# One-hot rows for eight tokens per instruction, as four interleaved pairs

## The chip, the cores and the metric

The kernel runs on one core of one Trainium2 chip. The metric is the device time of one execution in microseconds. A core has five engines that run beside each other, each with its own queue, in order: TensorE (PE, matmuls; its weight loads are shown as PEld), VectorE (DVE), ScalarE (ACT), GpSimd (POOL) and SyncE (SP, which here only issues transfers). They meet at semaphores. The lines L... are lines of the kernel before.

## The reference, cut to what matters

The kernel computes two transformer blocks on 512 tokens of width 1024. The change lies in the first block's expert layer, which picks 128 of 16,384 small experts per token (8 heads of 16) and sums their outputs:

```python
def peer_ffn(h, w_q, sub_keys, u, v):
    ...
    idx = jnp.take_along_axis(cand_idx, pos, axis=-1)     # i1 * 128 + i2
    g = jax.nn.softmax(top_s, axis=-1)
    ...
        ue = jnp.take(u, ib, axis=0)
        a = jnp.einsum('thkd,td->thk', ue, xb, preferred_element_type=jnp.float32)
        w = jax.nn.gelu(a) * gb
        ve = jnp.take(v, ib, axis=0)
        return jnp.einsum('thk,thkd->td', w.astype(ve.dtype), ve)
```

## The kernel before

The kernel gathers nothing. It multiplies all 16,384 rows of u with all tokens, weights each result with the gate of that expert for that token (zero for nearly all), and multiplies with all of v. An expert's number is a pair (i1, i2), each below 128. So the gates of one token are a 128 x 128 matrix, the sum over the 128 picks of an outer product of one-hot rows: a matmul over the picks, with a matrix of one-hot rows of i2 as the loaded operand and one-hot rows of i1, times the gate, as the moving one.

In `weights_of_pairs` (L1060 to L1085) VectorE builds these for one token at a time, the 128 picks on the partitions. L1073 compares `iotah` (0 to 127) with the token's column of `its` and gives `o2`; L1074 and L1076 compare with the other column and multiply by the high and the low half of the gate (`gts`), which give `g0` and `g1`. All three are 128x128 in 16 bits. Two matmuls at L1080 (PE, out `ax`) add up a token's matrix, four tokens share a PSUM bank (three `ax` banks), ScalarE copies the bank into `sg` at L1082, and after 32 tokens L1085 sends `sg` (2 MB) to the DRAM tensor `gdr`. The tiles `o2`, `g0` and `g1` hold four tokens and have four buffers each. In the trace they appear as o and g.

Beside it `up` (from L916) multiplies the tokens with u in units. A unit's weight is loaded by SyncE (L175, two buffers), rounded by ScalarE (L178, `wh`), its remainder `wl` is taken by GpSimd for the first units and by VectorE for the later ones (L179; `wh` and `wl` have two buffers), and 24 matmuls follow (L185 to L187, 128x512). VectorE takes the result out of PSUM (L924), ScalarE applies the gelu (L925).

`weave` (L1093) writes 128 steps of the one-hot work and 34 units in equal proportion; the last five units are written behind the last one-hot matmul. The final order of each engine's queue is set by a scheduler that places the instructions by its own estimate of times, so a change of a few instructions moves others. After this stretch, `gt` tiles are loaded from `gdr` (L1107, issued by GpSimd), multiplied into the activations (L1110), split (L190, L191) and multiplied with v (out `mm`, in `Wh`, `Wl`). In the same time `modulation` loads 96 pieces of `ada_w` into `araw` (L884, issued by GpSimd) and sums them on VectorE (L886, L888).

The tiles of the one-hot work lie in pools that are opened one behind the other in memory (`rp` with `its` and `gts`, `oh` at L1090, `stg` for `sg` at L1091) and given back before `wring`, `gpool` and `ad` (L1098 to L1100, `ad` holds `araw`) are opened over the same memory.

Of the kernel before, what the change touches and what calls it, by code (L numbers as in the profile page):

```python
# [11 lines left out]
F32 = mybir.dt.float32  # L12
F32R = mybir.dt.float32r
F16 = mybir.dt.float16
# [3 lines left out]
AF = mybir.ActivationFunctionType  # L18
ALU = mybir.AluOpType
# [3 lines left out]
GATE = 2.0 ** 15  # L23
# [104 lines left out]
def body(ctx, tc, nc, I, O):  # L128
    tensor, vector, scalar, gpsimd, sync = nc.tensor, nc.vector, nc.scalar, nc.gpsimd, nc.sync
# [20 lines left out]
    def ax_bank():  # L150
        return pax.tile([128, 512], F32, name="ax")
# [8 lines left out]
    for kt in range(8):  # L160
        t = resid.tile([128, S], F32, name=f"x{kt}")
# [164 lines left out]
    def proj_fm(h, chunk, evac, mt, eng=vector, w=None, bank=mm_bank):  # L326

        w = w or weight(chunk, eng=eng)
        ps = bank()
        for kt in range(8):  # L330
            mm3(ps, (w[0][:, kt], w[1][:, kt]), (h[0][kt], h[1][kt]), kt == 0, kt == 7)
        evac(mt, ps)

    def proj_fm4(h, chunks, evac, mts, eng=vector, steps=iter(())):

        banks = [mm_bank() for _ in range(4)]
        for c, ch in enumerate(chunks):
            w = weight(ch, 2, eng)
            for j in range(2):
                kt = 2 * c + j  # L340
                for i in range(4):
                    sl = slice(i * 128, (i + 1) * 128)
                    mm3(banks[i], (w[0][:, j, sl], w[1][:, j, sl]), (h[0][kt], h[1][kt]), kt == 0, kt == 7)
            next(steps, None)
        for i, mt in enumerate(mts):
            evac(mt, banks[i])
# [73 lines left out]
    with ExitStack() as st:  # L420
# [420 lines left out]
        for c in range(4):  # L841
            w = weight(I["w_up_hg"][c], 4)
            for m in range(2):
                mt = c * 2 + m
                g1 = gt3.tile([128, S], F32, name="g1")
# [58 lines left out]
    with ExitStack() as st:  # L904
# [9 lines left out]
        pr_ = Ctx()  # L914
# [24 lines left out]
        with ExitStack() as sr:  # L939
            rp = sr.enter_context(tc.tile_pool(name="rp", bufs=1))  # L940
            sr1 = sr.enter_context(ExitStack())
            rw = sr1.enter_context(tc.tile_pool(name="rw", bufs=2))
            iota = rp.tile([128, 128], F32, name="iota")
            gpsimd.iota(iota, pattern=[[1, 128]], base=0, channel_multiplier=0, allow_small_or_imprecise_dtypes=True)
            gs = rp.tile([128, 4, 8, 16], F32, name="gs")
            es = rp.tile([128, 4, 8, 16], F32, name="es")
            iotah = rp.tile([128, 128], F16, name="iotah")
            vector.tensor_copy(iotah, iota)

            its = rp.tile([128, 4, 2, 128], F32, name="its")  # L950
            gts = rp.tile([128, 2, 4, 128], F32, name="gts")
            gth = rp.tile([128, 4, 128], F16, name="gth")

            def top16(vals, idx, src, n):
                rest = rw.tile([128, n], F32, name=f"rest{n}")
# [57 lines left out]
            def norm_steps():  # L1013
                next(onorm.rms)
                yield
                next(onorm.rms)
                pr_.rrow = onorm.rrow(hp)
                yield

            def routing():  # L1020
                proj_fm4(H, [I["peer_wq"][c] for c in range(4)], evac_qp, range(4), gpsimd, norm_steps())
                yield
                for m in range(4, 16):
                    proj_fm(H, I["peer_wq"][m], evac_qp, m, vector if m > 10 else gpsimd)
                    if m % 2:
                        candidates((m - 5) // 2)
                    yield
                for hd in (6, 7):
                    candidates(hd)
                    yield  # L1030

                gv = gs.rearrange("p t h k -> p (t h) k")
                sh = [128, 32, 16]
                f1 = rw.tile([128, 4, 8, 16], F32, name="qs")
                fv = f1.rearrange("p t h k -> p (t h) k")
                vector.tensor_tensor(fv, gv, gv[:, :, 0:1].to_broadcast(sh), op=ALU.subtract)
                scalar.activation(gv, fv, AF.Exp)
                sm = rw.tile([128, 32], F32, name="sm", bufs=1)
                vector.tensor_reduce(sm, gv, axis=AX.X, op=ALU.add)
                vector.reciprocal(sm, sm)  # L1040
                vector.tensor_tensor(gv, gv, sm.unsqueeze(2).to_broadcast(sh), op=ALU.mult)

                ei = rw.tile([128, 4, 8, 16], I32, name="ss")
                ej = rw.tile([128, 4, 8, 16], I32, name="ss")
                vector.tensor_copy(ei, es)
                vector.tensor_scalar(ej, ei, 127, None, op0=ALU.bitwise_and)
                vector.tensor_scalar(ei, ei, 7, None, op0=ALU.logical_shift_right)
                vector.tensor_copy(f1, ei)
                vector.tensor_copy(es, ej)
                for t in range(4):  # L1050
                    tp = ax_bank()
                    for n, a in enumerate((f1, es, gs)):
                        tensor.transpose(tp[:, n * 128:(n + 1) * 128], a[:, t].rearrange("p h k -> p (h k)"), ident)
                    scalar.activation(its[:, t].rearrange("p z t -> p (z t)"), tp[:, 0:256], AF.Copy)

                    scalar.activation(gth[:, t], tp[:, 256:384], AF.Copy, scale=GATE)
                    vector.tensor_copy(gts[:, 0, t], gth[:, t])
                    vector.scalar_tensor_tensor(gts[:, 1, t], tp[:, 256:384], GATE, gth[:, t], op0=ALU.mult, op1=ALU.subtract)

            def weights_of_pairs(oh, stg):  # L1060

                for t in range(4):
                    for hb in range(4):
                        sg = stg.tile([128, 128, 32], F32, name="sg")
                        for n in range(0, 32, 4):
                            gps = ax_bank()
                            o2, g0, g1 = (oh.tile([128, 4, 128], F16, name=x) for x in ("o2", "g0", "g1"))
                            for i in range(4):  # L1070
                                c = hb * 32 + n + i
                                col = lambda x: x[:, c:c + 1]
                                vector.tensor_scalar(o2[:, i], iotah, col(its[:, t, 1]), None, op0=ALU.is_equal)  # L1073
                                vector.tensor_scalar(g0[:, i], iotah, col(its[:, t, 0]), col(gts[:, 0, t]),  # L1074
                                                     op0=ALU.is_equal, op1=ALU.mult)
                                vector.tensor_scalar(g1[:, i], iotah, col(its[:, t, 0]), col(gts[:, 1, t]),  # L1076
                                                     op0=ALU.is_equal, op1=ALU.mult)
                            for i in range(4):
                                for z, g in enumerate((g0, g1)):
                                    pr_.last = tensor.matmul(gps[:, i * 128:(i + 1) * 128], o2[:, i], g[:, i],  # L1080
                                                             start=z == 0, stop=z == 1)
                            scalar.activation(sg[:, :, n:n + 4].rearrange("p i t -> p t i"),  # L1082
                                              gps.rearrange("p (t i) -> p t i", t=4), AF.Copy, scale=1.0 / GATE)
                            yield
                        scalar.dma_start(gdr[t * 4 + hb], sg)  # L1085

            ups = up((*range(16 - SPILL, 16), *range(AHEAD)), gpsimd)
            weave((routing(), 16), (chain(idle(1), head(ups, UP1)), UP1))
            sr1.close()
            oh = sr.enter_context(tc.tile_pool(name="oh", bufs=4))  # L1090
            stg = sr.enter_context(tc.tile_pool(name="stg", bufs=2))  # L1091
            n = 8 * (AHEAD + SPILL) - UP1 - UP3
            weave((weights_of_pairs(oh, stg), 128), (head(ups, n), n))  # L1093
            with tc.issue_after(pr_.last.ins):
                for _ in ups:
# [729 lines left out]
```

## Time and profile before

| What | Value |
|---|---|
| median of three runs | 3665.86 us (3660.68 to 3665.9) |
| the profiled execution | 3660.42 us |
| its span in the trace | 3658.6 us |
| PE busy | 3453.6 us (94%) |
| DVE busy | 2568.2 us (70%) |
| ACT busy | 1382.4 us (38%) |
| POOL busy | 739.7 us (20%) |
| granted TensorE clock, mean | 0.968 |

The shares are means over the whole kernel; the stretch from 766 to 1156 us has other ones, and what the change is worth is read there. In the trace an instruction's recorded time reaches past the start of the next one on the same engine, so the price of an instruction in a full queue is the distance from its start to the next start.

### The profile page before, as it was taken

How to read it: one execution, taken by the hardware profiler on the slowest of the kernel's cores; microseconds unless marked ns; L12 is line 12 of the kernel's file. 1: busy time of each engine (PE TensorE's matmuls, PEld its weight loads, DVE VectorE, ACT ScalarE, POOL GpSimd, SP SyncE). 2: the span in 40 equal slices, each digit the busy share in tenths (PEclk: the TensorE clock that was granted, in tenths of full speed). 3: DMA queues.
4: the chain of work that ended last, by engine and by line, in shares of the span. 5: the costliest groups of instructions: out<-in, count | busy, mean ns of one | idle time of the engine just before them, and what ended most of it. 6: DMA issues, size and time to landing. Idle time of an engine off the chain costs nothing.

```text
span 3658.6 us, 45145 instructions
## 1 busy us (share of the span) xinstructions
PE 3453.6 (94%) x16848; PEld 2745.7 (75%) x16848; DVE 2568.2 (70%) x5258; ACT 1382.4 (38%) x1958; POOL 739.7 (20%) x703
## 2 busy tenths in 40 slices
PE   8999999998888899999999999978999998899998
PEld 7887787765466788788887888756786776787887
DVE  6687769999998777744445544697887776845444
ACT  4566532344444222222223323444343333233223
POOL 3221035532000311100001100063007552300000
PEclk9999999999798999999999999989999998899999
DMA  3211423334335677743346522311245446522222
GB/s 114 78 67 70 165 91 108 115 125 167 124 138 179 228 241 246 247 131 116 121 148 198 178 97 98 105 58 58 70 144 164 151 144 212 153 87 87 93 97 87
DMA packets 159467, 484.73 MB, mean 132 GB/s; under 512 B 16032, under 2 KB 50880, under 8 KB 154000
## 3 DMA queue, kind: packets, MB, share of 16 engines
q1 hardware_dynamic: 101008, 312.52, 24.9%
q0 software_dynamic: 26656, 97.56, 8.5%
q10 hardware_dynamic: 31584, 71.77, 5.4%
q8 instruction: 132, 2.16, 0.2%
q14 instruction: 87, 0.71, 0.1%
HBM read 407.41 MB, written 74.38 MB: 132 GB/s over the span
## 4 chain that ended last, share of the span: by engine, by line
PE 59%; DVE 22%; issue 7%; DMA 6%; POOL 3%; ACT 3%; ACTq 0%; SPq 0%; DVEq 0%; POOLq 0%
PE mm L185 18%; PE mm L186 18%; PE mm L187 18%; DMA araw<-ada_w 4%; DVE g L1074 4%; DVE g L1076 3%; DVE o L1073 2%; DVE wl L179 2%; DVE cacc L1503 2%; DVE aacc L888 1%; POOL wl L179 1%; DVE a L924 1%; ACT wh L178 1%; PE ax L707 1%; PE ax L1400 1%
## 5 line engine op out<-in xcount | busy, mean ns | idle before, releaser
L178 ACT ACTIVATE wh<-wr 128x1024 fp32r<-128x1024 f32 x516 | 546.0, 1059 | 1267.8 <-PE mm L187 907.3
L185 PE MATMUL mm<-hh,wl 128*128 128x512 f32 x2040 | 823.8, 404 | 30.9 <-POOL wl L179 15.3
L186 PE MATMUL mm<-hl,wh 128*128 128x512 f32 x2040 | 815.0, 400 | 0.0
L187 PE MATMUL mm<-hh,wh 128*128 128x512 f32 x2040 | 813.3, 399 | 0.0
L179 DVE TENSOR_TENSOR wl<-wr,wh 128x1024 fp32r<-128x1024 f32 x461 | 597.3, 1296 | 178.7 <-ACT wh L178 178.2
L185 PEld LDWEIGHTS mm<-hh,wl 128*128 128x128 f32 x2040 | 390.8, 192 | 128.0 <-DVE wl L179 20.6
L187 PEld LDWEIGHTS mm<-hh,wh 128*128 128x128 f32 x2040 | 390.4, 191 | 82.1 <-issue 1.6
L186 PEld LDWEIGHTS mm<-hl,wh 128*128 128x128 f32 x2040 | 391.0, 192 | 76.8 <-issue 0.2
L185 PE MATMUL mm<-Wh,wl 128*128 128x512 f32 x1024 | 404.9, 395 | 13.2 <-DVE wl L179 11.6
L187 PE MATMUL mm<-Wh,wh 128*128 128x512 f32 x1024 | 409.1, 400 | 0.0
L186 PE MATMUL mm<-Wl,wh 128*128 128x512 f32 x1024 | 405.1, 396 | 0.0
L1123 DVE TENSOR_TENSOR x<-x,mm 128x512 f32<-128x512 f32 x128 | 87.9, 687 | 252.8 <-PE mm L187 252.8
L185 PE MATMUL mm<-zh,wl 128*128 128x512 f32 x640 | 255.3, 401 | 3.1 <-DVE wl L179 3.1
L186 PE MATMUL mm<-zl,wh 128*128 128x512 f32 x640 | 255.1, 399 | 0.2 <-DVE zl L191 0.2
L187 PE MATMUL mm<-zh,wh 128*128 128x512 f32 x640 | 254.0, 397 | 0.0
L185 PEld LDWEIGHTS mm<-Wh,wl 128*128 128x128 f32 x1024 | 193.2, 189 | 62.1 <-DVE wl L179 14.2
L186 PEld LDWEIGHTS mm<-Wl,wh 128*128 128x128 f32 x1024 | 193.3, 189 | 49.2
L187 PEld LDWEIGHTS mm<-Wh,wh 128*128 128x128 f32 x1024 | 193.1, 189 | 44.8
L179 POOL TENSOR_TENSOR wl<-wr,wh 128x1024 fp32r<-128x1024 f32 x55 | 143.3, 2606 | 270.7 <-ACT wh L178 266.5
L1080 PE MATMUL ax<-g,o 128*128 128x128 f16 x1024 | 140.4, 227 | 44.3 <-DVE g L1074 31.6
L1074 DVE TENSOR_SCALAR g<-iotah,its,gts 128x128 f16<-128x128 f16 x512 | 179.7, 351 | 0.0
L1082 ACT ACTIVATE sg<-ax 128x512 f32<-128x512 f32 x128 | 131.0, 1082 | 117.2 <-PE ax L1080 115.9
(804 smaller groups left out, 5526.5 us busy)
## 6 DMA issues: line engine op xcount, KB each, us to landing
wr<-peer_u SPq DMA_DIRECT2D x128, 512.0 KB, 3.3
wr<-peer_v SPq DMA_DIRECT2D x128, 512.0 KB, 3.3
wr<-w_fc SPq DMA_DIRECT2D x128, 512.0 KB, 3.2
araw<-ada_w POOLq DMA_DIRECT2D x96, 512.0 KB, 4.3
gdr<-sg ACTq DMA_DIRECT2D x16, 2048.0 KB, 7.1
gt<-gdr POOLq DMA_DIRECT2D x32, 1024.0 KB, 8.1
spill<-a ACTq DMA_DIRECT2D x40, 256.0 KB, 2.0
a<-spill POOLq DMA_DIRECT2D x40, 256.0 KB, 5.0
```

The costliest lines, as they stand in the source:

```text
L178: scalar.activation(hi, raw, AF.Copy)
L179: eng.tensor_tensor(lo, raw, hi.bitcast(F32), op=ALU.subtract)
L185: tensor.matmul(out, wl, xh, start=start, stop=False)
L186: tensor.matmul(out, wh, xl, start=False, stop=False)
L187: tensor.matmul(out, wh, xh, start=False, stop=stop)
L1073: vector.tensor_scalar(o2[:, i], iotah, col(its[:, t, 1]), None, op0=ALU.is_equal)
L1074: vector.tensor_scalar(g0[:, i], iotah, col(its[:, t, 0]), col(gts[:, 0, t]), op0=ALU.is_equal, op1=ALU.mult)
L1076: vector.tensor_scalar(g1[:, i], iotah, col(its[:, t, 0]), col(gts[:, 1, t]), op0=ALU.is_equal, op1=ALU.mult)
L1080: pr_.last = tensor.matmul(gps[:, i * 128:(i + 1) * 128], o2[:, i], g[:, i], start=z == 0, stop=z == 1)
L1082: scalar.activation(sg[:, :, n:n + 4].rearrange("p i t -> p t i"), gps.rearrange("p (t i) -> p t i", t=4), AF.Copy, scale=1.0 / GATE)
L1123: vector.tensor_tensor(X[j], X[j], ps, op=ALU.add)
L1503: vector.scalar_tensor_tensor(cacc[m], pad, w, cacc[m], op0=ALU.mult, op1=ALU.add)
```

## The change

Eight tokens are handled by each instruction. `iotas` holds 0 to 127 four times, each number twice in a row, so that a tile [4, 128, 2] holds four pairs of tokens, and the two tokens of a pair alternate. Indices and gates are kept in 16 bits. VectorE now builds `o2` and a plain one-hot `eq` by comparing, and `g0` and `g1` by multiplying `eq` with the two halves of the gate: four TENSOR_TENSOR of 1,024 elements for eight tokens. The operand with a token's numbers is repeated 128 times between the pair index and the place in the pair. The matmuls read their token out of the pair with a step of two elements.

```diff
-            iotah = rp.tile([128, 128], F16, name="iotah")
-            vector.tensor_copy(iotah, iota)
+            iotas = rp.tile([128, 4, 128, 2], F16, name="iotas")
+            for n in range(4):
+                vector.tensor_copy(iotas[:, n], iota.unsqueeze(2).to_broadcast([128, 128, 2]))
-            its = rp.tile([128, 4, 2, 128], F32, name="its")
-            gts = rp.tile([128, 2, 4, 128], F32, name="gts")
-            gth = rp.tile([128, 4, 128], F16, name="gth")
+            its = rp.tile([128, 4, 2, 128], F16, name="its")
+            gts = rp.tile([128, 2, 4, 128], F16, name="gts")
...
-                            o2, g0, g1 = (oh.tile([128, 4, 128], F16, name=x) for x in ("o2", "g0", "g1"))
-                            for i in range(4):
-                                c = hb * 32 + n + i
-                                col = lambda x: x[:, c:c + 1]
-                                vector.tensor_scalar(o2[:, i], iotah, col(its[:, t, 1]), None, op0=ALU.is_equal)
-                                vector.tensor_scalar(g0[:, i], iotah, col(its[:, t, 0]), col(gts[:, 0, t]),
-                                                     op0=ALU.is_equal, op1=ALU.mult)
-                                vector.tensor_scalar(g1[:, i], iotah, col(its[:, t, 0]), col(gts[:, 1, t]),
-                                                     op0=ALU.is_equal, op1=ALU.mult)
...
-                                    pr_.last = tensor.matmul(gps[:, i * 128:(i + 1) * 128], o2[:, i], g[:, i],
-                                                             start=z == 0, stop=z == 1)
+                        for q in range(4):
+                            c = hb * 32 + q * 8
+                            sh = [128, 4, 128, 2]
+                            o2, eq, g0, g1 = (oh.tile(sh, F16, name=n) for n in ("o2", "eq", "g0", "g1"))
+                            col = lambda x: x[:, c:c + 8].rearrange("p (n i) -> p n i", i=2).unsqueeze(2).to_broadcast(sh)
+                            vector.tensor_tensor(o2, iotas, col(its[:, t, 1]), op=ALU.is_equal)
+                            vector.tensor_tensor(eq, iotas, col(its[:, t, 0]), op=ALU.is_equal)
+                            vector.tensor_tensor(g0, eq, col(gts[:, 0, t]), op=ALU.mult)
+                            vector.tensor_tensor(g1, eq, col(gts[:, 1, t]), op=ALU.mult)
+                            for h in range(2):
+                                gps = ax_bank()
+                                for i in range(4):
+                                    for z, g in enumerate((g0, g1)):
+                                        pr_.last = tensor.matmul(gps[:, i * 128:(i + 1) * 128], o2[:, 2 * h + i // 2, :, i % 2],
+                                                                 g[:, 2 * h + i // 2, :, i % 2], start=z == 0, stop=z == 1)
```

The numbers of the lines behind move by three (L1080 becomes L1076, L1107 becomes L1104), and the scheduler's order moves with them. VectorE's queue in the one-hot stretch, before (names as in the kernel, o for `o2`, g for `g0` and `g1`):

```order
1500 L1073 TENSOR_SCALAR o_8149<-iotah,its 128x128
1501 L1074 TENSOR_SCALAR g_8150<-iotah,its,gts 128x128
1502 L1076 TENSOR_SCALAR g_8151<-iotah,its,gts 128x128
1503 L1073 TENSOR_SCALAR o_8149<-iotah,its 128x128
1504 L1074 TENSOR_SCALAR g_8150<-iotah,its,gts 128x128
```

and after the change, in the same stretch:

```order
1187 L1070 TENSOR_TENSOR g_7656<-eq,gts 128x1024
1188 L1068 TENSOR_TENSOR o_7654<-iotas,its 128x1024
1189 L1071 TENSOR_TENSOR g_7657<-eq,gts 128x1024
1190 L1069 TENSOR_TENSOR eq<-iotas,its 128x1024
1191 L924 TENSOR_TENSOR a<-mm,rrow 128x512
```

Three instructions per token have become four per eight tokens, and the evacuation of a unit (L924) stands between them.

TensorE's queue in the same stretch, before (o is the loaded operand, g the moving one; L185 to L187 are a unit's matmuls):

```order
3402 L1080 LDWEIGHTS o_7877
3403 L1080 MATMUL ax<-g_7879,o_7877 128x128
3404 L186 MATMUL mm<-hl_4475,wh 128x512
3405 L1080 LDWEIGHTS o_7877
3406 L1080 MATMUL ax<-g_7878,o_7877 128x128
3407 L187 MATMUL mm<-hh_4474,wh 128x512
3408 L1080 LDWEIGHTS o_7877
```

and after, at the end of a run of 24 one-hot matmuls:

```order
4031 L1076 LDWEIGHTS o_8362
4032 L1076 MATMUL ax<-g_8365,o_8362 128x128
4033 L1076 LDWEIGHTS o_8362
4034 L1076 MATMUL ax<-g_8364,o_8362 128x128
4035 L1076 LDWEIGHTS o_8362
4036 L1076 MATMUL ax<-g_8365,o_8362 128x128
4037 L186 MATMUL mm<-hl_4436,wh 128x512
4038 L187 MATMUL mm<-hh_4435,wh 128x512
```

One-hot matmuls that stood between a unit's matmuls one or two at a time stand in runs of 24 (later also of 8 and 16), with 15 to 24 matmuls of units between the runs.

GpSimd's queue ahead of the expert layer, before (L873 to L884 are the loads of `modulation`):

```order
111 L873 DMA ca<-c 128x8
112 L876 DMA ab<-ada_b 128x96
113 L878 DMA ng<-norm_g 128x32
114 L884 DMA araw<-ada_w 128x1024 x10
115 L179 TENSOR_TENSOR wl<-wr,wh 128x1024
```

and after, where these loads now stand:

```order
259 L179 TENSOR_TENSOR wl<-wr,wh 128x1024 x22
260 L1104 DMA gt<-gdr 128x16x128 x2
261 L873 DMA ca<-c 128x8
262 L876 DMA ab<-ada_b 128x96
263 L878 DMA ng<-norm_g 128x32
264 L884 DMA araw<-ada_w 128x1024 x2
```

The ten loads of `ada_w` that stood ahead of the expert layer have moved behind the first two loads of `gt`.

## Rows read from the trace of the kernel before

**Rows 1.** Stretches: length, busy of PE, PEld, DVE, ACT, POOL, PEclk, DMA, GB/s.

```profile
766.50:952.00 185.50, 162.46 (x898) 104.47 (x896) 185.50 (x703) 83.09 (x91) 40.56 (x17) 0.94 0.38 141
952.00:1156.00 204.00, 171.88 (x934) 119.07 (x935) 203.26 (x888) 92.83 (x106) 0.00 (x0) 0.81 0.36 134
1156.00:1250.00 94.00, 81.95 (x343) 65.06 (x342) 64.45 (x75) 30.01 (x41) 30.44 (x26) 0.95 0.73 235
1250.00:1560.00 310.00, 306.35 (x1370) 249.59 (x1369) 235.57 (x276) 89.58 (x108) 48.44 (x83) 1.00 0.73 246
```

**Rows 2.** Waits of PE, 766.5 to 1156 us: total us, times, longest.

```profile
PE ax L1080 <- DVE g L1074: 31.6, 75, 2.3
```

**Rows 3.** In order of time, DVE and POOL near 850 us: start, us, instruction.

```profile
850.41 2.49 DVE L1074 TENSOR_SCALAR g<-iotah,its,gts 128x128 f16<-128x128 f16 x1
...
850.49 2.36 POOL L179 TENSOR_TENSOR wl<-wr,wh 128x1024 fp32r<-128x1024 f32 x1 [6.51 <-ACT wh L178]
...
852.82 0.30 DVE L1076 TENSOR_SCALAR g<-iotah,its,gts 128x128 f16<-128x128 f16 x1
853.04 0.24 DVE L1073 TENSOR_SCALAR o<-iotah,its 128x128 f16<-128x128 f16 x1
853.21 0.30 DVE L1074 TENSOR_SCALAR g<-iotah,its,gts 128x128 f16<-128x128 f16 x1
853.43 0.30 DVE L1076 TENSOR_SCALAR g<-iotah,its,gts 128x128 f16<-128x128 f16 x1
853.65 0.24 DVE L1073 TENSOR_SCALAR o<-iotah,its 128x128 f16<-128x128 f16 x1
```

**Rows 4.** Groups of DVE, 766.5 to 1156 us: count, busy us, mean ns, idle before.

```profile
L1073 DVE TENSOR_SCALAR o<-iotah,its 128x128 f16<-128x128 f16 x512 | 136.0, 266 | 3.1 <-PE ax L1053 3.1
L924 DVE TENSOR_TENSOR a<-mm,rrow 128x512 f32<-128x512 f32 x34 | 23.3, 684 | 0.3 <-PE mm L187 0.3
L179 DVE TENSOR_TENSOR wl<-wr,wh 128x1024 fp32r<-128x1024 f32 x17 | 20.8, 1222 | 0.4 <-ACT wh L178 0.4
```

**Rows 5.** In order of time, DVE: 32-bit instructions and what starts behind them.

```profile
1173.12 2.50 DVE L1110 TENSOR_TENSOR a<-a,gt 128x512 f32<-128x512 f32 x4 [4.75 <-DMA gt<-gdr]
1175.54 0.69 DVE L924 TENSOR_TENSOR a<-mm,rrow 128x512 f32<-128x512 f32 x1
...
1143.67 1.22 DVE L179 TENSOR_TENSOR wl<-wr,wh 128x1024 fp32r<-128x1024 f32 x1
1144.81 0.26 DVE L1073 TENSOR_SCALAR o<-iotah,its 128x128 f16<-128x128 f16 x1
```

**Rows 6.** L1010 of the routing: ns min/median/max, then its group.

```profile
L1010 DVE TENSOR_TENSOR eq<-eq,ce x32: 966/980/3177, 553.0 to 748.5; 128x800 f32<-128x800 f32 x32
...
L1010 DVE TENSOR_TENSOR eq<-eq,ce 128x800 f32<-128x800 f32 x32 | 42.1, 1357 | 0.0
```

**Rows 7.** In order of time, PE near 1022 us: a run of 24 one-hot matmuls.

```profile
1021.65 1.51 PE L1080 MATMUL ax<-g,o 128*128 128x128 f16 x24
1022.98 0.47 PE L185 MATMUL mm<-hh,wl 128*128 128x512 f32 x1
1023.29 0.39 PE L186 MATMUL mm<-hl,wh 128*128 128x512 f32 x1
1023.52 0.40 PE L187 MATMUL mm<-hh,wh 128*128 128x512 f32 x1
```

**Rows 8.** Weight loads: ns min/median/max of two lines, then two groups' means.

```profile
L1659 PEld LDWEIGHTS ax<-c_ident,hh x64: 132/133/173, 3063.4 to 3151.6; 128*64 128x64 f32 x64
...
L1684 PEld LDWEIGHTS mm<-U,Wk x512: 132/138/227, 3069.8 to 3164.8; 128*64 128x64 f32 x171
...
L1080 PEld LDWEIGHTS <-o 128*128 128x128 f16 x1024 | 70.6, 98 | 117.6 <-DVE g L1074 36.9 <-DVE o L1073 34.6 <-issue 18.5
...
L186 PEld LDWEIGHTS mm<-hl,wh 128*128 128x128 f32 x2040 | 391.0, 192 | 76.8 <-issue 0.2
```

**Rows 9.** The tile araw, 400 to 500 us: its loads.

```profile
L884 POOL DMA_DIRECT2D araw<-ada_w x10: 528/530/536, 413.1 to 441.4; - x10
```

**Rows 10.** The chain that ended last, around 1160 us: start, us, what.

```profile
1157.64 6.96 DMA gdr<-sg
...
1165.23 7.86 DMA gt<-gdr
```

More of the change, by code (lines that the diff above doesn't have):

```diff
@@ L1054, in routing @@
                     scalar.activation(its[:, t].rearrange("p z t -> p (z t)"), tp[:, 0:256], AF.Copy)
-                    scalar.activation(gth[:, t], tp[:, 256:384], AF.Copy, scale=GATE)
-                    vector.tensor_copy(gts[:, 0, t], gth[:, t])
-                    vector.scalar_tensor_tensor(gts[:, 1, t], tp[:, 256:384], GATE, gth[:, t], op0=ALU.mult, op1=ALU.subtract)
+                    scalar.activation(gts[:, 0, t], tp[:, 256:384], AF.Copy, scale=GATE)
+                    vector.scalar_tensor_tensor(gts[:, 1, t], tp[:, 256:384], GATE, gts[:, 0, t], op0=ALU.mult, op1=ALU.subtract)
             def weights_of_pairs(oh, stg):
@@ L1066, in weights_of_pairs @@
                         sg = stg.tile([128, 128, 32], F32, name="sg")
-                        for n in range(0, 32, 4):
-                            gps = ax_bank()
-                            o2, g0, g1 = (oh.tile([128, 4, 128], F16, name=x) for x in ("o2", "g0", "g1"))
-                            for i in range(4):
-                                c = hb * 32 + n + i
-                                col = lambda x: x[:, c:c + 1]
-                                vector.tensor_scalar(o2[:, i], iotah, col(its[:, t, 1]), None, op0=ALU.is_equal)
-                                vector.tensor_scalar(g0[:, i], iotah, col(its[:, t, 0]), col(gts[:, 0, t]),
-                                                     op0=ALU.is_equal, op1=ALU.mult)
-                                vector.tensor_scalar(g1[:, i], iotah, col(its[:, t, 0]), col(gts[:, 1, t]),
-                                                     op0=ALU.is_equal, op1=ALU.mult)
-                            for i in range(4):
-                                for z, g in enumerate((g0, g1)):
-                                    pr_.last = tensor.matmul(gps[:, i * 128:(i + 1) * 128], o2[:, i], g[:, i],
-                                                             start=z == 0, stop=z == 1)
-                            scalar.activation(sg[:, :, n:n + 4].rearrange("p i t -> p t i"),
-                                              gps.rearrange("p (t i) -> p t i", t=4), AF.Copy, scale=1.0 / GATE)
-                            yield
@@ new lines, in weights_of_pairs @@
+                        for q in range(4):
[13 more added lines that the diff above has]
+                                                                 g[:, 2 * h + i // 2, :, i % 2], start=z == 0, stop=z == 1)
+                                n = q * 8 + h * 4
+                                scalar.activation(sg[:, :, n:n + 4].rearrange("p i t -> p t i"),
+                                                  gps.rearrange("p (t i) -> p t i", t=4), AF.Copy, scale=1.0 / GATE)
+                                yield
```

## The prediction, made before the changed kernel was run

> **What bounds the kernel now.** Read the busy time by stretches first, then who waits in the stretch of the one-hot products, then VectorE in order of time, then its groups of instructions. The change touches one stretch, from 766.5 us, where the first one-hot row is built, to about 1156 us, where the last one-hot product is done: 389.5 us. VectorE is busy for 185.50 of the first 185.50 us and for 203.26 of the other 204.00 [rows 1]. TensorE is busy for 162.46 and 171.88, and its granted clock is 0.94 and then 0.81, so that part of this runs at 1.2 GHz in place of 2.4 [rows 1]. ScalarE is busy for 83 + 93 = 176 us. What TensorE's one-hot products wait for is the g rows of VectorE [rows 2].
>
> What fills VectorE is seen from starts, since the recorded times overlap. A token's three instructions start at 853.04 (o), 853.21 (g) and 853.43 (g), and the next token's o at 853.65: 0.61 us a token [rows 3]. GpSimd's weight subtraction runs from 850.49 for 2.36 us, and the VectorE instruction of 850.41, of a kind that elsewhere lasts 0.30, lasts 2.49, so that the next starts at 852.82 [rows 3]. Each of the 17 subtractions that GpSimd does in the first half [rows 1] thus costs VectorE 2.41 - 0.22 = 2.2 us. Sum: 512 x 0.61 = 312; 17 x 2.2 = 37; 34 evacuations L924 at 0.60 = 20 (four 128x512 instructions start at 1173.12, the next at 1175.54); 17 subtractions L179 of VectorE's own at 1.14 (1143.67 to 1144.81) = 19 [rows 4, 5]. That is 388 of 389.5 us: the stretch is VectorE's, and the one-hot rows are four fifths of it.
>
> **The change part by part.** It takes away 1,536 TENSOR_SCALAR of 128 elements and adds 64 groups of four TENSOR_TENSOR of 1,024, 256 instructions. No row shows a TENSOR_TENSOR on 16-bit operands, so its price is bounded. Above: the 32-bit one of 1,024 elements, one element a step, 1.14 us. Below: if two 16-bit elements go through in a step, it has the steps of a 32-bit one of 512 elements, 0.60 us [rows 5]. I take 0.60: the layout puts pairs of tokens side by side, so that the innermost run of the repeated operand is two neighbouring elements and every operand can be read in 4-byte words. A weak sign from the rows: 32-bit costs 0.06 us and 1.05 ns an element [rows 5], which for 128 elements would be 0.195, and the 16-bit o row takes 0.17 [rows 3].
>
> The Trainium skill speaks against the exchange here: VectorE: DVE Perf Modes, The perf-mode tier table, gives tensor_scalar on 16-bit data in SBUF four results a cycle and tensor_tensor only two. By its 1,224 ns for 2,048 elements, some 150 cycles of it fixed, the new instruction would last an estimated 0.69 us, and at 0.69 from start to start the sum below would come out some 12 us later. The trace agrees with that as the length of a record, but shows the next instruction starting earlier.
>
> VectorE then has 256 x 0.60 = 154, the same 20 and 19, and 17 x 2.4 = 41 for GpSimd (both inputs of the new instructions lie in SBUF, as with the routing's L1010, which lasts 0.97 undisturbed and up to 3.18 [rows 6]): 234 us in place of 388.
>
> **What is late next** is TensorE. It has 34 units of 24 matmuls, 0.23 us apart, and 1,024 one-hot products. A run of 24 of these can be seen, 1021.65 to 1022.98: 55 ns each at 2.4 GHz [rows 7]. After the change its queue holds them in such runs, 24 or 8 + 16, with 15 to 24 matmuls of units between, where before they stood mostly one or two at a time. A unit with its share of 30 products takes 24 x 0.228 + 30.1 x 0.055 = 7.1 us. VectorE takes for a unit 7.5 x 0.60 + 0.60 = 5.1, and 2.4 for GpSimd (7.5) or 1.14 of its own (6.3). So the first 17 units go at VectorE's 7.5, 128 us, and the other 17 at TensorE's 7.1, 121 us: 249 us if nobody waits needlessly. ScalarE's 176 us fit under it. But now two engines are within 6% of each other, with ScalarE and GpSimd in the chain of each weight (which has two buffers), and neither will always find its input. The next stretch, where several engines alternate, takes 94 us for 343 x 0.23 = 79 us of matmuls, 16% lost; the present one loses nothing against its bound [rows 1]. Between 0 and 16% I take 5%, as VectorE may run four tiles of rows, 32 tokens, ahead: 262 us. The gain in the stretch is 389.5 - 262 = 127.5 us.
>
> The products now read both operands with a step of two elements. Nearest row: the transposes of L1659, whose loaded operand has a step of eight 32-bit elements, load 64 columns in 133 ns, and the dense 64 columns of L1684 take 138 [rows 8]. So I take no cost; the upper end is that a 16-bit load with gaps goes like a 32-bit one, 192 ns for 98 [rows 8], and a product takes 110 ns.
>
> **Moved with it.** The row tiles grow from 12 to 32 KB a partition (four buffers each), and the sg tiles behind them, as I read the pools, now lie on the memory into which the first ten loads of ada_w went ahead, at 413 to 441 us [rows 9]; in the new order these stand behind the first gt loads. Ten loads of 512 KB at 246 GB/s are 21 us of transfers, in a stretch where the DMA share is 0.73 and TensorE is busy for 306 of 310 us [rows 1]: TensorE's matmuls cover them, unless a gt or weight load queues behind one. Bounds 0 to 21, taken 4. At the end of the one-hot stretch 7.0 us of store and 7.9 us of gt load are on the chain [rows 10]. In both orders five units, 27 us of matmuls, stand between the last product and the first weighted sum and cover them: 0 taken, though of the 15 us that TensorE loses up to 1250 some 10 could go or come. Building iotas is four instructions for one, at most 4 x 0.60 us: 1 taken. Sum: 127.5 - 4 - 1 = 122.5 us.
>
> **The rivals.**
> *The gaps in the operands cost TensorE* (upper end above): 7.1 becomes 8.8 us a unit, 34 x 8.8 = 299, with 5% 314 us, so 3,660 - 75 + 5 = 3,590. Against it the row of L1659. Chance 0.12.
> *The chain of the weights waits* (wh behind three sg of 1.08 us each, then GpSimd, while both buffers are full): 16% in place of 5%, 289 us: 3,565; with the clock falling in the waits, as now to 0.81, up to 3,600. Chance 0.10.
> *One element a step*: 256 x 1.14 = 292, with 80 of other work 372 us; VectorE still bounds, and 17 of gain less 5 gives 3,648. For it: no row shows the doubled rate. Against it: the layout. Chance 0.08.
> The Trainium skill has a rule on this, Vector Engine (DVE) Microarchitecture Reference, section 5.1: a two-source instruction takes two elements a cycle if all operands are 16-bit with an innermost step of 1, and one element read again and again (step 0) ran at one a cycle. By that rule the pairs give the forecast, and tokens laid out singly would have been this rival; no run here shows either so far.
> *Slower*: one element a step, and runs of only two elements cost the reader more time on top. It decides from the point where the 256 instructions take what the rows take now: (389.5 - 80) / 256 = 1.21 us each. L1010, both inputs in SBUF and one of them repeated, has a mean of 1.357 us for 800 elements, GpSimd's blocks included [rows 6]; 1,024 like that are 1.74 us, 445 us in all, with 39 of other work 484: 3,760. Chance 0.04.
>
> **How the numbers follow.** The profiled execution took 3660.42 us, 1.8 more than its span; it is at the low end of the three runs (median 3665.86), and the sum is made against it: 3660.4 - 122.5 = 3,538 us, chance 0.66. Its own range is 3,508 (249 us in the stretch, nothing displaced, 10 us of the tail gained) to 3,565. With the first two rivals, to 3,600, it holds 0.88 of the chance, so the range is 3,508 to 3,600. Under 0.2% (7 us) this kernel's time can't be told from no change: one element a step lands 12 us below, so that part of its chance, beside a worse tail, is same or slower. Faster 0.93, same 0.03, slower 0.04.
>
> **What would show it.** TENSOR_TENSOR of 1,024 16-bit elements starting 0.60 us apart (1.14: the third rival). Runs of one-hot products 55 ns apart (110: the first). VectorE's busy share of the stretch below 1 and TensorE's granted clock near 1.0 (lower: the waits of the second). The stretch some 262 us long, and the one after it, 1156 to 1560 now, as long as before to within 10 us. The forecast is wrong if an instruction takes 1.1 us or more, or if the stretch shrinks as said and the time behind it grows by what the loads of ada_w displace.

## The result, and the profile after

The changed kernel takes 3520.35 us (median of 4 runs, 3516.63 to 3524.76) against 3665.55 (4 runs, 3660.68 to 3665.9): 0.9607 of the time, 95% interval 0.9591 to 0.9624. It was forecast at 3,538 with a range of 3,508 to 3,600. The profiled execution of before lies at the low end of its runs (span 3658.6 us) and that of after at the high end (3522.4), so the traces show 136 of the 145 us between the medians.

| Part of the span, us | before | after |
|---|---|---|
| up to the first one-hot row | 766.5 | 767.3 |
| from there to the last one-hot product | 388.5 | 249.7 |
| behind it | 2503.6 | 2505.4 |

Where the last product starts, and before it the first (count, ns min/median/max, first and last start in us), the kernel before and then the changed one:

```profile
L1080 PE MATMUL ax<-g,o x1024: 216/219/290, 771.3 to 1154.7; 128*128 128x128 f16 x171
...
L1076 PE MATMUL ax<-g,o x1024: 217/218/235, 777.6 to 1016.9; 128*128 128x128 f16 x171
```

The last product of the kernel before ends at 1155.0, one microsecond ahead of the 1156 up to which [rows 1] and the prediction count, so the stretch was 388.5 us long and not 389.5. The whole gain is in this one stretch: 138.8 us, less 0.8 ahead of it and 1.8 behind. Both of these small terms lie within what the runs below scatter there. The busy times by stretches, which answer to [rows 1] (length, then busy of PE, PEld, DVE, ACT and POOL with instructions, PEclk, DMA share, GB/s):

```profile
767.30:895.00 127.70, 124.87 (x915) 103.40 (x914) 126.17 (x158) 88.59 (x98) 48.18 (x17) 1.00 0.59 217
895.00:1017.00 122.00, 122.00 (x913) 99.10 (x912) 100.51 (x151) 89.11 (x98) 0.00 (x0) 1.00 0.58 212
1017.00:1111.00 94.00, 81.29 (x346) 64.41 (x344) 64.62 (x75) 34.33 (x45) 35.51 (x31) 0.96 0.76 250
1111.00:1421.00 310.00, 306.93 (x1369) 249.82 (x1369) 233.57 (x273) 89.46 (x108) 49.52 (x85) 1.00 0.75 248
```

TensorE is now busy for 246.9 of 249.7 us with its clock at 1.00 (2.4 GHz) throughout, where it stood at 0.94 and 0.81; VectorE has room in the second part. The 94 us behind the stretch look as before. What the new instructions cost is read from starts, as in [rows 3] (VectorE of the changed kernel in order of time: start, us, instruction):

```profile
859.78 1.28 DVE L1069 TENSOR_TENSOR eq<-iotas,its 128x1024 f16<-128x1024 f16 x2
860.99 0.68 DVE L924 TENSOR_TENSOR a<-mm,rrow 128x512 f32<-128x512 f32 x1
861.59 2.30 DVE L1070 TENSOR_TENSOR g<-eq,gts 128x1024 f16<-128x1024 f16 x1
863.81 0.68 DVE L1068 TENSOR_TENSOR o<-iotas,its 128x1024 f16<-128x1024 f16 x1
864.41 0.68 DVE L1071 TENSOR_TENSOR g<-eq,gts 128x1024 f16<-128x1024 f16 x1
...
867.56 0.68 DVE L1070 TENSOR_TENSOR g<-eq,gts 128x1024 f16<-128x1024 f16 x1
868.16 0.68 DVE L1068 TENSOR_TENSOR o<-iotas,its 128x1024 f16<-128x1024 f16 x1
868.76 0.68 DVE L1071 TENSOR_TENSOR g<-eq,gts 128x1024 f16<-128x1024 f16 x1
869.36 0.68 DVE L924 TENSOR_TENSOR a<-mm,rrow 128x512 f32<-128x512 f32 x1
```

GpSimd's record beside the g of 861.59:

```profile
860.51 2.83 POOL L179 TENSOR_TENSOR wl<-wr,wh 128x1024 fp32r<-128x1024 f32 x1 [4.21 <-DMA wr<-peer_u]
```

From 867.56 on an instruction of 1,024 16-bit elements starts every 0.60 us, just as the 32-bit one of 512 elements (L924) does, and the record lasts 0.68: two elements go through in a step. The g of 861.59, which meets GpSimd's subtraction, lasts 2.30. And a run of one-hot products, as in [rows 7] (TensorE, in order of time):

```profile
881.34 1.55 PE L1076 MATMUL ax<-g,o 128*128 128x128 f16 x24
882.70 0.48 PE L185 MATMUL mm<-hh,wl 128*128 128x512 f32 x1
883.01 0.39 PE L186 MATMUL mm<-hl,wh 128*128 128x512 f32 x1
883.24 0.40 PE L187 MATMUL mm<-hh,wh 128*128 128x512 f32 x1
```

24 products take 1.36 us, 56.6 ns each, for 55.1 in the four runs of 24 of the kernel before (1.323 us). Who waits for whom in the stretch (total us, times, longest), beside [rows 2]:

```profile
ACT sg L1079 <- PE ax L1076: 32.4, 24, 2.1
...
DVE a L924 <- PE mm L187: 15.5, 9, 5.2
...
DVE g L1070 <- PE ax L1076: 6.3, 9, 1.9
...
PE ax L1076 <- ACT sg L1079: 1.6, 4, 0.7
...
PE mm L185 <- POOL wl L179: 1.1, 1, 1.1
```

The direction has turned: VectorE waits for TensorE, to finish a unit or to give back a row tile, and no one-hot product waits for rows any more. TensorE's own waits are the last two lines, 2.7 us in all, for a bank that ScalarE has to empty and for one remainder from GpSimd.

### The profile page after: what moved, and what is told of

Read it like the earlier page. It is cut to its first block, busy times and chain, and to the rows that moved or that the text cites. A ratio compares the mean times of both kernels' runs of the same rounds, so it can differ in the third digit from the quotient of the medians.

```text
span 3522.4 us, 43869 instructions
## 1 busy us (share of the span) xinstructions
PE 3368.6 (96%) x16848; PEld 2726.4 (77%) x16848; DVE 2406.5 (68%) x3977; ACT 1386.2 (39%) x1958; POOL 753.6 (21%) x703
## 4 chain that ended last, share of the span: by engine, by line
PE 67%; DVE 15%; issue 7%; DMA 6%; POOL 3%; ACT 3%; ACTq 0%; DVEq 0%; SPq 0%; POOLq 0%
PE mm L185 20%; PE mm L187 19%; PE mm L186 19%; DMA araw<-ada_w 5%; DVE cacc L1500 2%; DVE wl L179 2%; PE ax L1076 1%; DVE aacc L888 1%; POOL wl L179 1%; DMA gt<-gdr 1%; PE ax L707 1%; PE ax L1397 1%; PE po L596 1%; ACT wh L178 1%; DVE eq L1008 0%
## 5 line engine op out<-in xcount | busy, mean ns | idle before, releaser
L185 PE MATMUL mm<-hh,wl 128*128 128x512 f32 x2040 | 808.8, 397 | 22.5 <-POOL wl L179 16.5
L186 PE MATMUL mm<-hl,wh 128*128 128x512 f32 x2040 | 802.3, 393 | 0.0
L187 PE MATMUL mm<-hh,wh 128*128 128x512 f32 x2040 | 801.3, 393 | 0.0
L185 PEld LDWEIGHTS mm<-hh,wl 128*128 128x128 f32 x2040 | 384.6, 189 | 113.9 <-POOL wl L179 21.0
L187 PEld LDWEIGHTS mm<-hh,wh 128*128 128x128 f32 x2040 | 384.8, 189 | 80.1 <-issue 0.2
L185 PE MATMUL mm<-Wh,wl 128*128 128x512 f32 x1024 | 404.7, 395 | 15.0 <-DVE wl L179 12.6
L187 PE MATMUL mm<-Wh,wh 128*128 128x512 f32 x1024 | 408.0, 398 | 0.0
L185 PE MATMUL mm<-zh,wl 128*128 128x512 f32 x640 | 255.3, 401 | 3.1 <-DVE wl L179 3.1
L187 PE MATMUL mm<-zh,wh 128*128 128x512 f32 x640 | 254.1, 397 | 0.0
L185 PEld LDWEIGHTS mm<-Wh,wl 128*128 128x128 f32 x1024 | 192.6, 188 | 64.0 <-DVE wl L179 16.0
L187 PEld LDWEIGHTS mm<-Wh,wh 128*128 128x128 f32 x1024 | 192.6, 188 | 45.3
L179 POOL TENSOR_TENSOR wl<-wr,wh 128x1024 fp32r<-128x1024 f32 x55 | 151.7, 2759 | 278.1 <-ACT wh L178 268.7
L924 DVE TENSOR_TENSOR a<-mm,rrow 128x512 f32<-128x512 f32 x128 | 87.5, 684 | 125.6 <-PE mm L187 125.6
L1169 DVE SCALAR_TENSOR_TENSOR x<-mm,mod,x 128x512 f32<-128x512 f32 x72 | 53.9, 748 | 145.2 <-PE mm L187 145.0
L888 DVE SCALAR_TENSOR_TENSOR aacc<-araw,ca,aacc 128x1024 f32<-128x1024 f32 x84 | 110.8, 1319 | 55.8 <-DMA araw<-ada_w 55.7
```

The lines of the kernel that those rows point to most:

```text
L179: eng.tensor_tensor(lo, raw, hi.bitcast(F32), op=ALU.subtract)
L185: tensor.matmul(out, wl, xh, start=start, stop=False)
L186: tensor.matmul(out, wh, xl, start=False, stop=False)
L187: tensor.matmul(out, wh, xh, start=False, stop=stop)
L888: vector.scalar_tensor_tensor(acc, raw, ca[:, kt:kt + 1], acc, op0=ALU.mult, op1=ALU.add)
L924: vector.tensor_tensor(a, ps, pr_.rrow, op=ALU.mult)
```

## The experiments

Two questions: was it the price of VectorE's rows that was gained, and is it the pairs or the 16 bits that set that price? Then: which engine bounds the stretch now, and do the displaced loads of ada_w cost anything?

**The changed kernel again**, as the measure for the runs beside it.

> The changed kernel as it is, run beside the next three on the same chip, so that differences of a few microseconds can be read. Every theory: 3,516 to 3,525 us as in its four runs, the one-hot stretch (first one-hot row to last one-hot product) 250 us, and what lies behind it about 2,505 us.

Measured: 3521.72 us (3517.44 to 3526.96, 5 runs); stretch 764.1 to 1013.8, 249.7 us, 2505.6 behind it. As expected. The stretch:

```profile
764.10:1013.80 249.70, 246.90 (x1827) 202.48 (x1826) 226.08 (x308) 177.68 (x195) 47.99 (x17) 1.00 0.58 214
```

**Tokens laid out singly.**

```diff
-            iotas = rp.tile([128, 4, 128, 2], F16, name="iotas")
-            for n in range(4):
-                vector.tensor_copy(iotas[:, n], iota.unsqueeze(2).to_broadcast([128, 128, 2]))
+            iotas = rp.tile([128, 8, 128], F16, name="iotas")
+            for n in range(8):
+                vector.tensor_copy(iotas[:, n], iota)
...
-                            sh = [128, 4, 128, 2]
+                            sh = [128, 8, 128]
...
-                            col = lambda x: x[:, c:c + 8].rearrange("p (n i) -> p n i", i=2).unsqueeze(2).to_broadcast(sh)
+                            col = lambda x: x[:, c:c + 8].unsqueeze(2).to_broadcast(sh)
...
-                                        pr_.last = tensor.matmul(gps[:, i * 128:(i + 1) * 128], o2[:, 2 * h + i // 2, :, i % 2],
-                                                                 g[:, 2 * h + i // 2, :, i % 2], start=z == 0, stop=z == 1)
+                                        pr_.last = tensor.matmul(gps[:, i * 128:(i + 1) * 128], o2[:, 4 * h + i],
+                                                                 g[:, 4 * h + i], start=z == 0, stop=z == 1)
```

> Eight tokens per instruction as in the changed kernel, same count of instructions, elements and bytes, but laid out token by token ([8, 128]): the repeated operand is then one 16-bit element read 128 times, and TensorE reads its operands without gaps. Theory, the pairs are what lets two elements through in a step: 1.14 us per instruction in place of 0.60, VectorE's sum 372 us, the stretch 372 or a little more, 3,640 to 3,655 us. Rival, the 16 bits alone do it: 0.60 us, the stretch 250, 3,520. And with operands without gaps a run of 24 products takes 1.33 us if the gaps cost the 0.06 seen in the changed kernel (1.39), else 1.39.

Measured: 3642.74 us (3641.58 to 3649.09), 0.9945 of before, interval 0.9926 to 0.9963. VectorE in order of time:

```profile
894.00 1.21 DVE L1070 TENSOR_TENSOR g<-eq,gts 128x1024 f16<-128x1024 f16 x1
895.13 1.21 DVE L1068 TENSOR_TENSOR o<-iotas,its 128x1024 f16<-128x1024 f16 x1
896.27 1.21 DVE L1071 TENSOR_TENSOR g<-eq,gts 128x1024 f16<-128x1024 f16 x1
```

TensorE there, a run of 24 products and a matmul of the unit beside it:

```profile
895.70 1.51 PE L1076 MATMUL ax<-g,o 128*128 128x128 f16 x24
897.02 0.47 PE L187 MATMUL mm<-hh,wh 128*128 128x512 f32 x1
```

And the stretch as a whole:

```profile
768.10:1133.80 365.70, 282.64 (x1826) 225.30 (x1824) 364.27 (x308) 176.91 (x197) 49.19 (x17) 0.87 0.39 148
```

The same 16-bit elements in the same number now start 1.14 us apart, the price of 32-bit ones [rows 5]; VectorE is busy for 364.3 of 365.7 us and TensorE's clock is at 0.87. So the pairs are worth 116 of the 139 us of the stretch, and eight tokens in an instruction without them 23. The rival, that the 16 bits do it, falls. Against the gain stands the price of the gaps: without them a run of 24 takes 1.32 us, as in the kernel before, and with them 1.36, 1.5 ns a product, 1.5 us over all 1,024.

**Larger groups, old instructions.** A tile holds eight tokens and two banks follow on it, as after; the rows come from TENSOR_SCALAR, one token each, with indices and gates in 32 bits as before. The cut shows the edit against the changed kernel.

```diff
...
-                            vector.tensor_tensor(o2, iotas, col(its[:, t, 1]), op=ALU.is_equal)
-                            vector.tensor_tensor(eq, iotas, col(its[:, t, 0]), op=ALU.is_equal)
-                            vector.tensor_tensor(g0, eq, col(gts[:, 0, t]), op=ALU.mult)
-                            vector.tensor_tensor(g1, eq, col(gts[:, 1, t]), op=ALU.mult)
+                            for i in range(8):
+                                vector.tensor_scalar(o2[:, i], iotah, col(its[:, t, 1], i), None, op0=ALU.is_equal)
+                                vector.tensor_scalar(g0[:, i], iotah, col(its[:, t, 0], i), col(gts[:, 0, t], i),
+                                                     op0=ALU.is_equal, op1=ALU.mult)
+                                vector.tensor_scalar(g1[:, i], iotah, col(its[:, t, 0], i), col(gts[:, 1, t], i),
+                                                     op0=ALU.is_equal, op1=ALU.mult)
...
```

> The instructions of the kernel before (three TENSOR_SCALAR per token), in tiles of eight tokens and with two banks per tile as in the changed kernel. Theory, the price of VectorE's rows is the gain: 0.61 us a token, the stretch 388 us as before, 3,655 to 3,670 us. Rival, the larger groups (longer runs of one-hot products, the scheduler's other order, the higher clock) bring part of the gain: the stretch below 370 us.

Measured: 3666.08 us (3659.64 to 3669.61), 1.0006 of before, interval 0.9995 to 1.0016. The stretch:

```profile
765.00:1154.00 389.00, 333.30 (x1835) 223.65 (x1834) 388.57 (x1589) 176.37 (x198) 40.56 (x17) 0.87 0.38 137
```

Nothing is left of the gain (the last product ends at 1151.9, 387.0 us for 388.5). The grouping by itself is worth nothing, and the scheduler interleaves the products one and two at a time as before. So the long runs and the clock of 1.00 didn't come here without the cheaper rows. Where long runs did come without them, in the singles (up to 24 products), the clock was 0.87 and all of the gain 23 us. How much of the rest hangs on the clock of 1.00 no run separates.

**GpSimd's part of the weight subtractions**, none of it in the stretch, and all of it:

```diff
-        AHEAD, SPILL, UP1, UP3, UPV = 3, 5, 25, 5, 44
+        AHEAD, SPILL, UP1, UP3, UPV = 3, 5, 25, 5, 25
```

> The weight subtractions that GpSimd does for the first 17 units of the stretch go to VectorE (1.14 us each, and no blocks of 2.4). Theory of the two halves (the prediction's sum): the first half goes at VectorE's 7.5 us a unit because of GpSimd, so without it every unit goes at TensorE's 7.1 and the stretch falls from 250 to about 243, the time by 6 to 7 us. Rival, TensorE bounds all the stretch after the first 50 us: 0 to 3 us less.

```diff
-        AHEAD, SPILL, UP1, UP3, UPV = 3, 5, 25, 5, 44
+        AHEAD, SPILL, UP1, UP3, UPV = 3, 5, 25, 5, 59
```

> All 34 units of the stretch have their subtraction on GpSimd, in place of the first 19. Theory of the two halves: the second half then goes at VectorE's 7.5 us a unit too, the stretch grows from 250 to about 257, the time by 6 to 7 us. Rival, TensorE bounds it and VectorE has room: 0 to 3 us more, VectorE's busy time in the second half up by some 20 us all the same.

Measured: 3523.25 us (3515.85 to 3528.16) and 3519.95 (3517.89 to 3527.48), against 3521.72 for the changed kernel beside them: no difference. The two parts of the stretch without GpSimd:

```profile
765.60:893.00 127.40, 126.71 (x929) 102.29 (x928) 118.96 (x182) 89.66 (x100) 0.00 (x0) 1.00 0.61 219
893.00:1014.00 121.00, 121.00 (x902) 98.01 (x900) 96.03 (x144) 86.84 (x95) 0.00 (x0) 1.00 0.57 211
```

And with it for all units:

```profile
764.10:891.00 126.90, 124.08 (x912) 102.74 (x911) 125.53 (x157) 87.79 (x98) 48.28 (x17) 1.00 0.59 218
891.00:1014.40 123.40, 122.98 (x916) 99.91 (x916) 114.44 (x137) 89.80 (x99) 39.55 (x16) 1.00 0.56 209
```

VectorE's busy time goes from 215 us (without) to 240 (with), and the stretch from 248.4 to 250.3. The theory of two halves, with VectorE bounding the first, falls: it asked for 6 to 7 us either way. TensorE bounds the stretch in both, and VectorE's 25 us fit into its waits. The 25 us also give the price of a remainder on GpSimd: 33 of them stand in place of VectorE's own at 1.14, 0.76 more each, so one costs VectorE 1.9 us.

**VectorE relieved, TensorE relieved.**

```diff
...
-                            vector.tensor_tensor(g1, eq, col(gts[:, 1, t]), op=ALU.mult)
...
-                                    for z, g in enumerate((g0, g1)):
+                                    for z, g in enumerate((g0, eq)):
```

> The low half of the gate is not built: the instruction for g1 is left out and the second product takes eq in its place, so the sum is another. VectorE has 64 instructions of 0.60 us less, 38 us; TensorE's work is the same. Theory, TensorE bounds the stretch: it stays at 247 to 250 us, the time within 5 us of the changed kernel. Rival, VectorE still bounds a part: up to 19 us less (half of 38).

```diff
-                                    for z, g in enumerate((g0, g1)):
+                                    for z, g in enumerate((g0,)):
...
-                                                                 g[:, 2 * h + i // 2, :, i % 2], start=z == 0, stop=z == 1)
+                                                                 g[:, 2 * h + i // 2, :, i % 2], start=True, stop=True)
```

> The product with the low half of the gate is left out (g1 is built and not used): 512 one-hot products in place of 1,024, VectorE's work the same. Theory, TensorE bounds the stretch: 512 x 0.058 = 30 us less for TensorE, and the stretch falls to VectorE's 235 or a little above, 10 to 15 us less. Rival, VectorE bounds it: no difference beyond 3 us.

Measured: 3515.55 us (3513.72 to 3518.89) and 3516.96 (3510.2 to 3518.25). The stretch without the second product's rows (g1):

```profile
766.70:1012.50 245.80, 245.80 (x1827) 202.04 (x1825) 184.75 (x244) 177.66 (x195) 41.23 (x17) 1.00 0.59 218
```

And with one product for each token:

```profile
767.70:1007.00 239.30, 225.21 (x1315) 174.95 (x1313) 228.13 (x307) 175.20 (x194) 54.85 (x17) 0.98 0.60 223
```

TensorE's waits in that stretch, which are all of its idle time there:

```profile
PE ax L1076 <- ACT sg L1079: 7.5, 8, 2.3
PE mm L185 <- POOL wl L179: 6.3, 3, 2.4
```

38 us less of VectorE's work shortens the stretch by 3.9 us, and TensorE is then busy without a gap; 29 us less of TensorE's (512 x 56.6 ns) shortens it by 10.4. So TensorE bounds the stretch of the changed kernel. What bounds it some 10 us below is less clear: VectorE is then busy for 228 of 239 us, but what TensorE waits for is ScalarE's emptying of banks and GpSimd's remainders. In the times the 10 us are not cleanly seen: the second run takes 0.9589 of the kernel before beside it (interval 0.9565 to 0.9613), the changed kernel 0.9609 of its own (0.9595 to 0.9623). Behind the stretch the profiled executions take 2509 us with one product and 2499 without g1, for 2505 in the changed kernel; neither edit touches that part.

**Four tokens per instruction.**

```diff
...
-                        for q in range(4):
-                            c = hb * 32 + q * 8
-                            sh = [128, 4, 128, 2]
+                        for q in range(8):
+                            c = hb * 32 + q * 4
+                            sh = [128, 2, 128, 2]
...
```

> Four tokens per instruction, as two pairs: 512 instructions of 512 elements in place of 256 of 1,024. By the slope of the rows (0.06 us and half of 1.05 ns an element) each starts 0.33 us after the one before, 169 us in all for 154, so VectorE's sum rises from 234 to 249 us, and TensorE's stays 242. Theory, TensorE bounds the stretch: 250 to 254 us there. The row tiles shrink to 16 KB, so the early loads of ada_w come back here too: if they cost what the run with small tiles seemed to show, 3,530 to 3,540 us in all, else 3,518 to 3,526.

Measured: 3533.98 us (3524.75 to 3544.44). VectorE in order of time:

```profile
880.33 0.41 DVE L1070 TENSOR_TENSOR g<-eq,gts 128x512 f16<-128x512 f16 x1
880.67 0.41 DVE L1068 TENSOR_TENSOR o<-iotas,its 128x512 f16<-128x512 f16 x1
881.00 0.41 DVE L1071 TENSOR_TENSOR g<-eq,gts 128x512 f16<-128x512 f16 x1
```

The stretch:

```profile
767.70:1016.00 248.30, 247.10 (x1826) 201.94 (x1825) 240.02 (x564) 178.03 (x195) 57.08 (x17) 1.00 0.58 216
```

0.335 us for 512 elements: the fixed part is 0.07 us and the rest 0.52 ns an element, so eight tokens per instruction save 0.07 x 256 = 18 us of VectorE's work over four, and the stretch doesn't need them: 248.3 us. The time is longer all the same, outside the stretch, and the next two runs are about that.

**The loads of ada_w.** First brought back in the changed kernel with smaller row tiles, then displaced in the kernel before with an unused tile.

```diff
-                            o2, eq, g0, g1 = (oh.tile(sh, F16, name=n) for n in ("o2", "eq", "g0", "g1"))
+                            o2, eq, g0, g1 = (oh.tile(sh, F16, name=n, bufs=1 if n == "eq" else 3) for n in ("o2", "eq", "g0", "g1"))
```

> The row tiles take 20 KB a partition in place of 32 (three buffers for o2, g0, g1, one for eq), so that the sg tiles end below the memory of araw and the first ten loads of ada_w stand ahead of the expert layer again, at about 410 us. The prediction's term: the displaced loads cost 4 us behind the stretch, bounds 0 to 21; by the trace of the changed kernel 2.8. So the part behind the stretch 3 to 4 us shorter, the stretch itself unchanged if VectorE needs no more than 24 tokens ahead, up to 5 us longer if it does. Rival, the displaced loads cost nothing and the 2.8 us are scatter: no difference.

```diff
             iotah = rp.tile([128, 128], F16, name="iotah")
+            pad = rp.tile([128, 4096], F32, name="pad")
+            vector.memset(pad[:, 0:1], 0.0)
```

> The kernel before with an unused tile of 16 KB a partition ahead of the one-hot tiles: nothing is computed otherwise, but the sg tiles now lie over the memory of araw, and the ten first loads of ada_w stand behind the first gt loads, as in the changed kernel. By the prediction's term (displaced loads cost 0 to 21 us, 4 taken): 3,667 to 3,672 us, the stretch 389 us as before. By the run with small tiles, where the loads were brought back and the time was 13 us longer: the displaced loads are no cost and perhaps a gain, 3,650 to 3,664 us.

Measured: 3534.37 us (3530.77 to 3541.44), 12.7 more than the changed kernel beside it, and 3664.98 us (3658.51 to 3670.98), 1.0002 of before, interval 0.9992 to 1.0012. The stretch with the small tiles, and ahead of it the 100 us of the early loads:

```profile
770.20:1019.80 249.60, 246.91 (x1827) 202.05 (x1825) 231.91 (x308) 177.74 (x195) 44.23 (x17) 1.00 0.58 214
...
400.00:500.00 100.00, 95.84 (x433) 77.25 (x433) 70.09 (x101) 42.73 (x61) 9.35 (x14) 1.00 0.45 148
```

The same 100 us of the changed kernel run beside it:

```profile
400.00:500.00 100.00, 100.00 (x458) 81.90 (x456) 65.03 (x98) 41.17 (x58) 5.21 (x3) 1.00 0.34 107
```

The stretch is the same to 0.1 us, so 24 tokens ahead are enough. The loss lies ahead of it (6.1 us later) and behind it (2516.4 us for 2505.6). With the early loads TensorE does 433 matmuls in those 100 us, without them 458, but this dip alone isn't the loss ahead of the stretch: the kernel before does 438 with the loads early and 457 with the loads displaced, and its first one-hot row comes at 766.5 us both times. In the other kernels the first row comes at 764.1 to 768.1 us, with early loads or without. Displaced, in the kernel before, the same loads make no difference beyond the 0.12% of the interval; the kernel with the old instructions in larger groups, whose tiles displace them too (the first at 1168.6 us), agrees. So displacing them costs at most some 4.4 us, and nothing is seen; having them early is no gain. Why both kernels with early loads and small tiles (this one and that with four tokens, 2516.2 us) are some 10 us longer behind the stretch stays open. In part it is lost from 94 to 404 us behind it, where TensorE does 1,339 and 1,347 matmuls, against 1,366 and 1,369 in the two traces of the changed kernel; but the kernel before, with early loads, does 1,370. The scheduler's order differs in every one of these kernels, and no run separated the loads from the order.

## Why the prediction was right, point by point

*The bound.* VectorE's rows bounded the stretch, and cheaper rows shortened it; the kernel with the old instructions in the new groups shows that the grouping didn't, and the singles that 16-bit indices and gates didn't.

*The price of an instruction.* 0.60 us was taken between 0.60 and 1.14, and 0.60 it is. The layout was the reason given, and the tokens laid out singly, at 1.14, show that the layout decides; that it does so by reads of 4-byte words no run shows. The third rival was priced at 3,648 us; the kernel that realizes it takes 3,643. On the rule of the Trainium skill (Vector Engine (DVE) Microarchitecture Reference, section 5.1) the traces agree with both halves: 16-bit operands with an innermost step of 1 went two to a step, although the repeated operand's runs are only two elements long, and a single element read again and again went at one. The estimate of 0.69 us from the Trainium skill (VectorE: DVE Perf Modes, The perf-mode tier table) is the length of the record (0.68), and not the distance between starts (0.60). The exchange of four results a cycle for two, against which the prediction quoted that table, was a gain all the same: a token's rows took 0.61 us [rows 3] and take 4 x 0.60 / 8 = 0.30 now. What the price of the old instructions was made of no run shows.

*The step that was off: the allowance of 5% for waits.* The stretch was put at 249 us without waits and at 262 with them; it measured 249.7, with TensorE busy for all but 2.8 us of it. So some 3 us of waits stand against the 12.5 taken, and that term is most of the 13.7 us by which the forecast gain (122.5) fell short of the one in the traces (136.2). 32 tokens of rows ahead, and 24 too, hide nearly all that one engine waits for another.

*Right by its sum, wrong by its halves.* The 249 us were made of 128 us at VectorE's pace, because of GpSimd's blocks, and 121 at TensorE's. The two parts did measure 127.7 and 122.0 us, but the runs without GpSimd and with it throughout show that TensorE bounds both. Two terms were off. GpSimd's block was put at 2.4 us on top of the instruction that it meets. From start to start such an instruction takes 2.4 us (the mean of the 17 in the trace; 2.22 for the one shown at 861.59), but its own 0.60 is in that and was counted twice. With the 1.8 that is left VectorE's first half goes at 5.1 + 1.8 = 6.9 us a unit, under the 7.1 taken for TensorE, which then bounds both halves. TensorE's work, 242 us by those 7.1, was put too low: it is busy for 246.9, with 1.5 ns more a product (1.5 us) and some 0.08 us at each of 61 changes from products to units (5 us; the first unit matmul behind a run takes 0.31 us for 0.23). One price was too high and the other too low, and that the 249 us and each half came out was luck.

*The gaps in the operands*: taken as nothing, 1.5 us measured. The first rival, 110 ns a product, falls. *The loads of ada_w*: 4 us taken; the 1.8 in the traces is within the scatter, and the run of their own shows none. *The tail*: 0 taken; TensorE's 94 us behind the stretch are 81.3 busy for 82.0. *iotas*: 1 us taken; its four casts start 0.2 us apart at 497 us, and the 0.8 us ahead of the stretch is less than the 3.2 between the two traces of the changed kernel.

## What to carry to other kernels

Where one small operand is repeated over a long run, let a pair of its 16-bit elements lie innermost: a two-input VectorE instruction then took two elements a step here, and with a single repeated element one, which was worth 116 us. Price an instruction by the distance between starts in a full queue, and bound an unseen 16-bit one by the 32-bit rows of half and of equal length. When a bound of 390 us falls, add up the engine behind it from its own runs first; here it stood at 247, so 38 us less on VectorE were worth 3.9.

## What the runs showed that was not expected

Two engines within a tenth of each other (247 us busy and 227) left the later one idle for only 2.8 us, with three to four row tiles between them. A step of two 16-bit elements in both operands costs a 128-column product only 1.5 ns of 55. And edits of a few lines moved a kernel of 3.5 ms by some 10 us in places that they don't touch, as the small tiles and the four tokens show (by the scheduler's new order or by the early loads, which no run separates), about as much as the last effects that one would like to measure here.
